# Another order of the seven block products, and of their loads, in the gate and up products of the feed-forward network

## The chip, the cores and the metric

The kernel runs on one core of a Trainium2 chip. The metric is the device time of one execution in microseconds (us). TensorE is called PE in the rows, its weight loads PEld, VectorE DVE, ScalarE ACT, GpSimd POOL and SyncE SP.

## The reference

Two post-norm decoder layers over 512 tokens of width 1024, all in fp32. Each layer has a token mixer (dilated attention beside retention) and then the feed-forward network that this case is about:

```
def _swiglu(x, w_gate, w_up, w_down):
    h = jax.nn.silu(jnp.einsum('bsd,df->bsf', x, w_gate)) * jnp.einsum('bsd,df->bsf', x, w_up)
    return jnp.einsum('bsf,fd->bsd', h, w_down)
...
for l in range(DEPTH):
    mix = _hybrid_mixer(...)
    x = _layer_norm(ALPHA * x + mix, ln1_g[l], ln1_b[l])
    ffn = _swiglu(x, w_ffn_gate[l], w_ffn_up[l], w_ffn_down[l])
    x = _layer_norm(ALPHA * x + ffn, ln2_g[l], ln2_b[l])
```

The hidden width is 2816, which is 22 column blocks of 128.

## The kernel before

Every fp32 product is made from fp32r halves: an operand is cast to a high part (`whi`, ScalarE, line 323), and the low part is what the cast left over (`wlo`, VectorE, line 329). `mm3` then issues three matmuls: high by high, high by low, low by high.

The feed-forward network walks over pairs of column blocks, f = 0, 2, ..., 20. The pair f = 0 is a plain product (`ffn_plain`). The ten others (`ffn_pair`) treat gate and up together as the right half of a 2 x 2 block product: the tokens are halved (256 each) and the 1024 inputs are halved (512 each), so that A11, A12, A21, A22 are blocks of x, B11 and B21 are the two halves of the up weights, and B12 and B22 those of the gate weights. In Winograd's form seven block products do instead of eight:

| product | left | right | running sum in PSUM | what its eviction does |
|---|---|---|---|---|
| M1 | A11 | B11 | A (first) | ScalarE copies A to `sn` (line 1050) |
| M2 | A12 | B21 | X (alone) | VectorE adds X to the copy of M1 |
| M5 | S1 | P1 = B11 + B12 | C (first) | ScalarE copies C |
| M3 | S4 | B22 | C | VectorE subtracts, silu, product, `put` to `ht` |
| M6 | S2 | P2 = P1 + B22 | A | ScalarE copies A |
| M7 | S3 | P3 = B12 + B22 | A | VectorE subtracts from the copy of M5, silu |
| M4 | A22 | P4 = P2 + B21 | A | VectorE multiplies, `put` to `ht` |

Signs are left to the sums S1 to S4 of x, which are made once a layer (`x_sums`). A product is 24 matmuls of 256 columns (two 128-column halves of the weights, four 128-row blocks, three matmuls each). Chain A is one PSUM tile that M1, M6, M7 and M4 add to, so M6 can't write it until M1 has been copied out, and so on; chain C holds M5 and then M3.

The right sides: five loads of 512 KB a call on SP's queue. P1 and P3 are loaded, and the gate block is then added in place by an accumulating DMA that GpSimd issues (line 314). P2 and P4 are VectorE additions in place into P1's buffer (line 340). Raw loads rotate through 8 buffers (`rawp`), `whi` and `wlo` through 4 each (`wp`), PSUM tiles through 8. So the cast for one product waits until the product four ahead of it in the order has left its `whi`.

`ORDER` sets the order of the products and so the order in which `Right` prepares the weights: `operands` casts the next product's right side before the current one's matmuls. A scheduler then places the instructions in each engine's queue; it may pull matmuls of one product between those of another. The pairs are run in three parts (f = 2 and 4; 6 to 12; 14 to 20), and after each part the down product of what it made follows (`xstat`, 512-column matmuls named `ps<-...,ht`).

Of the kernel before, what the change touches and what calls it, by code (L numbers as in the profile page):

```python
# [18 lines left out]
P = 128  # L19
# [34 lines left out]
def hybrid_kernel(ctx, tc, x, rel_bias, w_in, b_in, w_attn_proj, w_ret_proj, w_out,  # L54
# [28 lines left out]
    def mm3(ps, ah, al, bh, bl, start, stop):  # L83
        mm(ps, ah, bh, start, False)
        mm(ps, ah, bl, False, False)
        mm(ps, al, bh, False, stop)

    def psum(name="px"):
        return psm.tile([P, S], F32, tag="mm", name=name)

    def hilo(src, hi, lo):
        act.copy(out=hi, in_=src)  # L92
        dve.tensor_tensor(out=lo, in0=src, in1=hi.bitcast(F32), op=ALU.subtract)  # L93
# [4 lines left out]
    def work(name):  # L98
        return wk.tile([P, S], F32, tag="w2", name=name)

    def rows(w):
        return w.rearrange("(k p) c -> p k c", p=P)
# [4 lines left out]
    def load(src, a, b):  # L107
        v = view(raw(), a, b)
        nc.sync.dma_start(v, src)
        return v  # L110

    def unit(v):
        a, b = v.shape[1], v.shape[2]
        h = view(wp.tile([P, 1024], F32R, tag="whi", name="whi"), a, b)
        l = view(wp.tile([P, 1024], F32R, tag="wlo", name="wlo"), a, b)
        hilo(v, h, l)
        return h, l
# [15 lines left out]
    def tick(us):  # L133

        if side:
            credit[0] += rate[0] * us
            while side and credit[0] >= 1.0:
                credit[0] -= 1.0
                side.popleft()()
# [88 lines left out]
    def wstat(us, q):  # L228

        need(*range(NI))  # L230
        ps = psum("ps")
        for k in range(KD):
            h, l = part_of(us, k, q)
            mm3(ps, h, l, xh[:, k], xl[:, k], k == 0, k == KD - 1)
            tick(STEP)
        return ps
# [41 lines left out]
    def tail_units(raws):  # L278

        out_ = []  # L280
        for j, r in enumerate(raws):
# [12 lines left out]
    ORDER = ((1, "A11", "B11"), (2, "A12", "B21"), (5, "S1", "P1"), (3, "S4", "B22"),  # L294
             (6, "S2", "P2"), (7, "S3", "P3"), (4, "A22", "P4"))
    CHAIN = {1: "A", 6: "A", 7: "A", 4: "A", 2: "X", 5: "C", 3: "C"}
    FIRST = (1, 2, 5)

    class Right:

        def __init__(self, src, shapes):
            self.src, self.shapes, self.t = src, shapes, {}

        def load(self, *names):
            for n in names:
# [24 lines left out]
        def begin(self, n):  # L333

            if n == "B11":
                self.load("B11", "B21", "P1", "P3", "B22")
            elif n in ("P2", "P4"):
                for u in range(len(self.shapes)):
                    r = self.t["P1", u]
                    dve.tensor_tensor(out=r, in0=r, in1=self.t["B22" if n == "P2" else "B21", u], op=ALU.add)  # L340
            return self.high(n)

        def operands(self):

            ahead = self.begin("B11")
            for i in range(len(ORDER)):
                now, low = ahead
                low()
                ahead = self.begin(ORDER[i + 1][2]) if i + 1 < len(ORDER) else None
                yield now  # L350

    def x_left(an, j, ts_):

        if an[0] == "S":
            o_ = xs[:, SN.index(an)]
            return o_[:, 0, j, ts_], o_[:, 1, j, ts_]
        k = j + (4 if an[2] == "2" else 0)
        o = 256 if an[1] == "2" else 0
        t_ = slice(o + ts_.start, o + ts_.stop)
        return xh[:, k, t_], xl[:, k, t_]  # L360

    def tall(right, n, left, ev, bias_=None):
# [3 lines left out]
        for (i, an, bn), units in zip(ORDER, right.operands()):  # L366
            ks = [(u, k) for u in units for k in range(u[0].shape[1])]
            c = CHAIN[i]
            for a in range(2):
                fresh = i in FIRST  # L370
                if fresh:
# [17 lines left out]

    def wide(right, left, ev):  # L390

        ps = {}
        for (i, an, bn), ((h, l),) in zip(ORDER, right.operands()):
            c = CHAIN[i]
            if i in FIRST:
                ps[c] = psum("ps")
            for q in range(2):
                cs = slice(q * P, (q + 1) * P)
                for k in range(4):
                    ah, al = left(an, k, slice(0, 256))  # L400
                    mm3(ps[c][:, q * 256:(q + 1) * 256], h[:, k, cs], l[:, k, cs], ah, al,
                        i in FIRST and q == 0 and k == 0, k == 3)
                    tick(STEP / 2)
            if i != 3:
                ev(i, ps[c])
            if i == 6:
                ev(3, ps["C"])
            yield

    def run(g):  # L410
        for _ in g:
            pass
# [204 lines left out]
    def layer(ly, cp):  # L617
# [197 lines left out]
        with stage("ret") as rp:  # L815
# [93 lines left out]
            for dp in range(KD // 2):  # L909
                sg = []  # L910
                for b, c in enumerate((C_GA, C_GB)):
                    us = pair_units(w_l, c + dp * 256)
                    t = slot("sg", F32)
                    for e in range(2):
                        ps = wstat(us, e)
# [3 lines left out]
                h, l = unit(load(wa_l[:, :, dp * 256:(dp + 1) * 256], NG, 256))  # L919
                if dp == KD // 2 - 1:  # L920
                    drain()
                for e in range(2):
                    cs = slice(e * P, (e + 1) * P)
                    ps = psum("ps")
# [39 lines left out]
        with stage("mp") as mp:  # L964
# [10 lines left out]
            for dp in range(KD // 2):  # L975
# [9 lines left out]
                for hh, (h, l) in enumerate(us):  # L985
                    for e in range(2):
                        cs = slice(e * P, (e + 1) * P)
                        for t in range(4):
                            k = 4 * hh + t
# [28 lines left out]
        wg_l, wu_l, wd_l = rows(w_ffn_gate[ly]), rows(w_ffn_up[ly]), rows(w_ffn_down[ly])  # L1018
# [15 lines left out]

        def ffn_pair(f, o_):

            def src(b, u):
                k = 4 if b[1] == "2" else 0
                return (wg_l if b[2] == "2" else wu_l)[:, k:k + 4, f * P:f * P + 256]

            sn = {}

            def put(v, ts_):
                hilo(v, o_[:, 0, :, ts_], o_[:, 1, :, ts_])

            def ev(i, ps):
                p2 = ps.rearrange("p (q t) -> p q t", q=2)
                if i in (1, 5, 6):
                    sn[i] = work("sn").rearrange("p (q t) -> p q t", q=2)
                    act.copy(out=sn[i], in_=p2)  # L1050
                elif i == 2:
                    dve.tensor_tensor(out=sn[1], in0=p2, in1=sn[1], op=ALU.add)
                elif i == 3:
                    v = sn[6]
                    dve.tensor_tensor(out=v, in0=p2, in1=v, op=ALU.subtract)
                    act.activation(out=v, in_=v, func=AF.Silu)
                    dve.tensor_tensor(out=v, in0=v, in1=sn[1], op=ALU.mult)
                    put(v, slice(0, 256))
                elif i == 7:
                    dve.tensor_tensor(out=sn[5], in0=sn[5], in1=p2, op=ALU.subtract)  # L1060
                    act.activation(out=sn[5], in_=sn[5], func=AF.Silu)
                elif i == 4:
                    v = sn[5]
                    dve.tensor_tensor(out=v, in0=v, in1=p2, op=ALU.mult)
                    put(v, slice(256, 512))

            run(wide(Right(src, [(4, 256)]), x_left, ev))

        for part, (f0, f1) in enumerate(FPARTS):
            ht = []  # L1070
# [89 lines left out]
```

## Time and profile before

| what | value |
|---|---|
| median of 3 runs | 2224.86 us (2223.46 to 2225.05) |
| the profiled execution, its own time | 2224.68 us |
| its span, first to last instruction | 2222.9 us |
| PE busy | 2184.1 us, 98% of the span |
| PEld / DVE / ACT / POOL busy | 85% / 61% / 43% / 11% |
| granted PE clock, mean | 0.998 |
| mean DMA rate | 147 GB/s |

The span and the time of the same execution differ by 1.8 us, which lies before the first and behind the last instruction. A row of the timeline gives start, duration, engine, line, operation and, in brackets, how long the engine had been idle and what ended that. Matmuls overlap in the pipeline, so their rate is read from start to start, and not from their durations.

### The profile page before, as it was taken

How to read it: one execution, taken by the hardware profiler on the slowest of the kernel's cores; microseconds unless marked ns; L12 is line 12 of the kernel's file. 1: busy time of each engine (PE TensorE's matmuls, PEld its weight loads, DVE VectorE, ACT ScalarE, POOL GpSimd, SP SyncE). 2: the span in 40 equal slices, each digit the busy share in tenths (PEclk: the TensorE clock that was granted, in tenths of full speed). 3: DMA queues.
4: the chain of work that ended last, by engine and by line, in shares of the span. 5: the costliest groups of instructions: out<-in, count | busy, mean ns of one | idle time of the engine just before them, and what ended most of it. 6: DMA issues, size and time to landing. Idle time of an engine off the chain costs nothing.

```text
span 2222.9 us, 31189 instructions
## 1 busy us (share of the span) xinstructions
PE 2184.1 (98%) x12330; PEld 1884.7 (85%) x12330; DVE 1352.1 (61%) x1971; ACT 946.8 (43%) x1517; POOL 233.5 (11%) x280
## 2 busy tenths in 40 slices
PE   8999999999999999999999999999999999999998
PEld 7877788888888898989898778888888889899896
DVE  5643677875245675646676447777843357666575
ACT  4444544545333253525245445444543234444350
POOL 3110011100000100000040100111000001010001
PEclk9999999999999999999999999999999999999999
DMA  8944266455656356556269343666455562565551
GB/s 226 238 124 103 63 157 170 132 141 157 207 179 190 85 144 141 161 133 152 86 160 243 105 94 85 151 164 157 130 175 192 185 189 64 160 149 155 128 152 38
DMA packets 293300, 325.92 MB, mean 147 GB/s; under 512 B 22478, under 2 KB 231522, under 8 KB 293025
## 3 DMA queue, kind: packets, MB, share of 16 engines
q1 hardware_dynamic: 223488, 244.62, 36.7%
q0 software_dynamic: 42384, 66.52, 15.4%
q10 hardware_dynamic: 27280, 12.80, 2.0%
q8 instruction: 96, 1.57, 0.3%
q14 instruction: 52, 0.42, 0.1%
HBM read 298.09 MB, written 28.53 MB: 147 GB/s over the span
## 4 chain that ended last, share of the span: by engine, by line
PE 80%; issue 10%; DMA 5%; DVE 3%; ACT 2%; POOL 1%; SPq 0%; POOLq 0%; DVEq 0%; ACTq 0%
PE ps L81 72%; PE px L81 6%; DMA raw<-in_w_in 3%; DVE wlo L329 1%; ACT whi L323 1%; PE px L526 1%; PE px L858 1%; DVE wlo L93 0%; POOL ry L124 0%; DMA rb<-in_b_in 0%; PE px L169 0%; DMA exd<-pk 0%; DVE xtok L951 0%; DMA exd<-wb 0%; ACT whi L92 0%
## 5 line engine op out<-in xcount | busy, mean ns | idle before, releaser
L81 PE MATMUL ps<-xh,whi 128*128 128x512 f32 (+1 forms) x1600 | 562.6, 353 | 5.9 <-ACT whi L92 3.3
L81 PE MATMUL ps<-xh,wlo 128*128 128x512 f32 (+1 forms) x1600 | 546.5, 342 | 10.5 <-DVE wlo L329 9.0
L81 PE MATMUL ps<-xl,whi 128*128 128x512 f32 (+1 forms) x1600 | 544.9, 341 | 0.2 <-DVE xl L93 0.2
L329 DVE TENSOR_TENSOR wlo<-raw,whi 128x1024 fp32r<-128x1024 f32 (+1 forms) x308 | 349.4, 1136 | 183.4 <-ACT whi L323 180.3
L323 ACT CAST whi<-raw 128x1024 fp32r<-128x1024 f32 (+1 forms) x308 | 300.4, 979 | 303.1 <-PE ps L81 176.9
L93 DVE TENSOR_TENSOR wlo<-raw,whi 128x1024 fp32r<-128x1024 f32 (+2 forms) x194 | 232.4, 1200 | 300.1 <-ACT whi L92 299.4
L81 PEld LDWEIGHTS ps<-xh,wlo 128*128 128x128 f32 x1600 | 302.7, 189 | 48.8 <-DVE wlo L329 11.5
L81 PEld LDWEIGHTS ps<-xh,whi 128*128 128x128 f32 x1600 | 302.2, 190 | 46.4 <-issue 6.4
L81 PEld LDWEIGHTS ps<-xl,whi 128*128 128x128 f32 x1600 | 303.8, 190 | 29.0 <-DVE xl L93 1.0
L92 ACT CAST whi<-raw 128x1024 fp32r<-128x1024 f32 (+2 forms) x194 | 198.7, 1031 | 285.4 <-PE ps L81 216.5
L81 PE MATMUL ps<-xs,whi 128*128 128x256 f32 (+1 forms) x1536 | 315.1, 302 | 0.0
L81 PEld LDWEIGHTS ps<-xs,whi 128*128 128x128 f32 x1536 | 248.7, 191 | 13.8 <-ACT sn L1050 3.5
L81 PE MATMUL ps<-xs,wlo 128*128 128x256 f32 (+1 forms) x768 | 229.9, 301 | 0.0
L81 PE MATMUL ps<-whi,xs 128*128 128x512 f32 (+1 forms) x768 | 220.0, 360 | 2.8 <-ACT whi L323 1.6
L81 PE MATMUL ps<-whi,ht 128*128 128x512 f32 x576 | 178.8, 390 | 0.0
L81 PEld LDWEIGHTS ps<-whi,xs 128*128 128x128 f32 x768 | 137.7, 188 | 23.6 <-ACT whi L323 2.4
L81 PEld LDWEIGHTS ps<-xs,wlo 128*128 128x128 f32 x768 | 146.5, 191 | 5.4 <-DVE wlo L329 0.4
L81 PE MATMUL ps<-wlo,xs 128*128 128x512 f32 (+1 forms) x384 | 138.3, 360 | 2.7 <-DVE wlo L329 2.5
L81 PEld LDWEIGHTS ps<-whi,ht 128*128 128x128 f32 x576 | 107.4, 188 | 21.4
L314 POOL DMA_DIRECT2D raw<-in_w_ffn_gate x40 | 51.9, 1298 | 675.8 <-DMA raw<-in_w_ffn_up 378.3
L81 PE MATMUL ps<-wlo,ht 128*128 128x512 f32 x288 | 112.8, 392 | 0.3
L81 PE MATMUL ps<-whi,xh 128*128 128x512 f32 (+1 forms) x288 | 103.5, 359 | 1.4 <-DVE sn L453 1.4
(179 smaller groups left out, 2862.3 us busy)
## 6 DMA issues: line engine op xcount, KB each, us to landing
raw<-in_w_in SPq DMA_DIRECT2D x144, 512.0 KB, 4.1
raw<-in_w_ffn_up SPq DMA_DIRECT2D x64, 512.0 KB, 4.5
raw<-in_w_ffn_gate SPq DMA_DIRECT2D x44, 512.0 KB, 3.8
raw<-in_w_ffn_down SPq DMA_DIRECT2D x44, 512.0 KB, 3.7
raw<-in_w_ffn_gate POOLq DMA_DIRECT2D x40, 512.0 KB, 6.4
raw<-in_w_in SPq DMA_DIRECT2D x72, 256.0 KB, 5.0
raw<-in_w_in POOLq DMA_DIRECT2D x32, 512.0 KB, 8.6
raw<-in_w_ret_proj SPq DMA_DIRECT2D x32, 512.0 KB, 4.0
```

The costliest lines, as they stand in the source:

```text
L81: pe.matmul(ps, lhsT=a, rhs=b, start=start, stop=stop, skip_group_check=True)
L92: act.copy(out=hi, in_=src)
L93: dve.tensor_tensor(out=lo, in0=src, in1=hi.bitcast(F32), op=ALU.subtract)
L314: pool.dma_start(r, self.src({"P1": "B12", "P3": "B22"}[n], u), accum_op=ALU.add)
L323: act.copy(out=h, in_=src)
L329: dve.tensor_tensor(out=l, in0=src, in1=h.bitcast(F32), op=ALU.subtract)
L526: pe.transpose(px[:, (2 + j) * P:(3 + j) * P], s[:, hh, j * P:(j + 1) * P], ident)
L858: pe.transpose(px[:, t * P:(t + 1) * P], ys[i][:, t * P:(t + 1) * P], ident)
```

## The change

The wide form gets an order and an order of loads of its own. For nine of the ten pairs of a layer the products come as M1, M5, M6, M2, M7, M3, M4; for f = 2, M1, M2, M5, M6, M3, M7, M4, because the sums S1 to S4 are then still being made. The loads come as B11, P1, B22, P3, B21 in all ten. Each product's eviction is now called right behind its product; before, that of M3 was called behind M6. The other users of `Right` (the `tall` form) keep their order.

```diff
+    WIDE = tuple(ORDER[i] for i in (0, 2, 4, 1, 5, 3, 6))
+    WIDE1 = tuple(ORDER[i] for i in (0, 1, 2, 4, 3, 5, 6))
...
-        def __init__(self, src, shapes):
-            self.src, self.shapes, self.t = src, shapes, {}
+        def __init__(self, src, shapes, order=ORDER, loads=("B11", "B21", "P1", "P3", "B22")):
+            self.src, self.shapes, self.order, self.loads, self.t = src, shapes, order, loads, {}
...
             if n == "B11":
-                self.load("B11", "B21", "P1", "P3", "B22")
+                self.load(*self.loads)
...
+    def pair_right(w1, w2, c, order=WIDE):
+
+        def src(b, u):
+            k = 4 if b[1] == "2" else 0
+            return (w2 if b[2] == "2" else w1)[:, k:k + 4, c:c + 256]
+
+        return Right(src, [(4, 256)], order, ("B11", "P1", "B22", "P3", "B21"))
...
-        for (i, an, bn), ((h, l),) in zip(ORDER, right.operands()):
+        for (i, an, bn), ((h, l),) in zip(right.order, right.operands()):
...
-            if i != 3:
-                ev(i, ps[c])
-            if i == 6:
-                ev(3, ps["C"])
-            yield
+            ev(i, ps[c])
...
-            run(wide(Right(src, [(4, 256)]), x_left, ev))
+            wide(pair_right(wu_l, wg_l, f * P, WIDE1 if f == 2 else WIDE), x_left, ev)
```

On PE, where one pair call of the second part (running sum A in `ps_7606`) meets the next (`ps_7837`). Right sides here: `whi_7696` is P2, `whi_7724` is P3, `whi_7830` is the next call's B11. Before:

```order
L81 MATMUL ps_7606<-xs_81,wlo_7697 128x256
L81 MATMUL ps_7606<-xs_81,whi_7696 128x256 x2
L81 MATMUL ps_7606<-xs_81,wlo_7697 128x256
L81 MATMUL ps_7837<-xh_79,whi_7830 128x256
L81 MATMUL ps_7837<-xl_80,whi_7830 128x256
L81 MATMUL ps_7837<-xh_79,wlo_7831 128x256
L81 MATMUL ps_7837<-xh_79,whi_7830 128x256
L81 MATMUL ps_7837<-xl_80,whi_7830 128x256
L81 MATMUL ps_7837<-xh_79,wlo_7831 128x256
L81 MATMUL ps_7837<-xh_79,whi_7830 128x256
L81 MATMUL ps_7606<-xs_81,whi_7724 128x256 x2
L81 MATMUL ps_7606<-xs_81,wlo_7725 128x256
```

And now, where `whi_7757` is P4:

```order
L81 MATMUL ps_7606<-xl_80,whi_7757 128x256
L81 MATMUL ps_7606<-xh_79,wlo_7758 128x256
L81 MATMUL ps_7606<-xh_79,whi_7757 128x256
L81 MATMUL ps_7606<-xl_80,whi_7757 128x256
L81 MATMUL ps_7606<-xh_79,wlo_7758 128x256
L81 MATMUL ps_7837<-xh_79,whi_7830 128x256
L81 MATMUL ps_7837<-xl_80,whi_7830 128x256
L81 MATMUL ps_7837<-xh_79,wlo_7831 128x256
```

Before, 7 matmuls of the next call's M1 stood between M6 and M7 of the running call, and 8 more between M7 and M4; in the same way M6 was cut in two (13 and 11) around M3. Now the seven products of these calls follow each other whole, 24 matmuls each, and the next call's M1 stands behind M4.

On ACT, the casts and PSUM copies of the same call. Before (`ps_7667` is chain C; 7664 is B22, 7760 P4):

```order
L1050 COPY sn_7631<-ps_7606 128x512
L323 CAST whi_7696<-raw_7591 128x1024
L323 CAST whi_7724<-raw_7594 128x1024
L323 CAST whi_7760<-raw_7591 128x1024
L1050 COPY sn_7692<-ps_7667 128x512
L323 CAST whi_7830<-raw_7818 128x1024
L323 CAST whi_7834<-raw_7820 128x1024
L1050 COPY sn_7751<-ps_7606 128x512
L1056 ACTIVATE sn_7751<-sn_7751 128x512
```

And now (`ps_7638` is chain C; 7696 is P3, 7726 B22, 7757 P4, 7830 and 7834 the next call's B11 and P1, 7866 its P2):

```order
L325 CAST whi_7696<-raw_7594 128x1024
L1053 COPY sn_7631<-ps_7606 128x512
L325 CAST whi_7726<-raw_7592 128x1024
L1053 COPY sn_7663<-ps_7638 128x512
L325 CAST whi_7757<-raw_7589 128x1024
L1053 COPY sn_7693<-ps_7606 128x512
L325 CAST whi_7830<-raw_7818 128x1024
L325 CAST whi_7834<-raw_7820 128x1024
L1064 ACTIVATE sn_7663<-sn_7663 128x512
L325 CAST whi_7866<-raw_7820 128x1024
```

The copies of M1, M5 and M6 (into `sn_7631`, `sn_7663`, `sn_7693`) now each stand behind one cast, and the next call's B11, whose cast stood ahead of M6's copy, is now cast behind it.

On POOL, in layer 0, where the first layer norm's reciprocal roots (`ry`) meet the accumulating loads of f = 2 and f = 4. Before:

```order
L314 DMA raw_6688<-in_w_ffn_gate 128x4x256
L314 DMA raw_6691<-in_w_ffn_gate 128x4x256
L124 TENSOR_TENSOR ry_6258<-ve_6257,mhalf_76 128x1
L314 DMA raw_6933<-in_w_ffn_gate 128x4x256
L124 TENSOR_TENSOR ry_6297<-ve_6296,mhalf_76 128x1
```

And now:

```order
L316 DMA raw_6686<-in_w_ffn_gate 128x4x256
L316 DMA raw_6691<-in_w_ffn_gate 128x4x256
L316 DMA raw_6931<-in_w_ffn_gate 128x4x256
L124 TENSOR_TENSOR ry_6258<-ve_6257,mhalf_76 128x1
L124 TENSOR_TENSOR ry_6297<-ve_6296,mhalf_76 128x1
```

The accumulating load of f = 4's P1 (`raw_6933` before, `raw_6931` now) has moved from behind the first root to in front of it.

## Rows read from the trace of the kernel before

**Rows 1.** The page, part 4: the chain that ended last, by engine.

```profile
PE 80%; issue 10%; DMA 5%; DVE 3%; ACT 2%; POOL 1%; SPq 0%; POOLq 0%; DVEq 0%; ACTq 0%
```

**Rows 2.** The chain over the second part, layer 0: start us, us, what.

```profile
874.91 15.99 PE ps L81 x131
890.90 3.15 issue
894.05 1.05 ACT whi L323
...
895.13 1.24 DVE wlo L329
...
896.41 15.99 PE ps L81 x131
```

**Rows 3.** TensorE's timeline in that stretch: start us, us, instruction, idle before.

```profile
890.68 0.77 PE L81 MATMUL ps<-xs,whi 128*128 128x256 f32 x3
891.29 0.28 PE L81 MATMUL ps<-xs,wlo 128*128 128x256 f32 x1
...
895.37 0.28 PE L81 MATMUL ps<-xl,whi 128*128 128x256 f32 x1
896.41 0.39 PE L81 MATMUL ps<-xh,wlo 128*128 128x256 f32 x1 [0.75 <-DVE wlo L329]
896.63 0.28 PE L81 MATMUL ps<-xh,whi 128*128 128x256 f32 x1
896.75 0.27 PE L81 MATMUL ps<-xl,whi 128*128 128x256 f32 x1
...
900.93 0.37 PE L81 MATMUL ps<-xh,whi 128*128 128x256 f32 x1
901.14 0.28 PE L81 MATMUL ps<-xl,whi 128*128 128x256 f32 x1
```

**Rows 4.** Windows view of one call: us, each engine's busy us (x instructions), clock, DMA.

```profile
874.91:896.41 21.50, 20.74 (x169) 20.31 (x169) 15.22 (x16) 10.90 (x16) 2.58 (x2) 1.00 0.72 172
```

**Rows 5.** ScalarE's timeline in the same call.

```profile
889.36 1.05 ACT L323 CAST whi<-raw 128x1024 fp32r<-128x1024 f32 x1 [1.83 <-PE ps L81]
890.31 0.58 ACT L1050 COPY sn<-ps 128x512 f32<-128x512 f32 x1
```

**Rows 6.** TensorE's timeline where the first part's down product begins.

```profile
820.67 0.62 PE L81 MATMUL ps<-whi,ht 128*128 128x512 f32 x2
821.36 0.50 PE L81 MATMUL ps<-wlo,ht 128*128 128x512 f32 x1
```

**Rows 7.** Groups by line and shape: busy us, mean ns of one | idle before.

```profile
L329 DVE TENSOR_TENSOR wlo<-raw,whi 128x1024 fp32r<-128x1024 f32 x252 | 307.3, 1222 | 159.2 <-ACT whi L323 156.5
...
L323 ACT CAST whi<-raw 128x1024 fp32r<-128x1024 f32 x252 | 262.9, 1047 | 256.4 <-PE ps L81 151.1 <-issue 76.0 <-ACT whi L323 11.4
...
L340 DVE TENSOR_TENSOR raw<-raw 128x1024 f32<-128x1024 f32 x72 | 87.8, 1220 | 1.5
...
L314 POOL DMA_DIRECT2D raw<-in_w_ffn_gate x40 | 51.9, 1298 | 675.8 <-DMA raw<-in_w_ffn_up 378.3 <-DVE ht L93 96.1 <-DVE wlo L329 95.6
...
L1050 ACT COPY sn<-ps 128x512 f32<-128x512 f32 x60 | 34.8, 581 | 3.9 <-PE ps L81 3.9
```

**Rows 8.** Timelines of VectorE and ScalarE in the call f = 2, layer 0.

```profile
784.84 0.68 DVE L1032 TENSOR_TENSOR sl<-sl,ps 128x512 f32<-128x512 f32 x1
...
787.06 0.59 ACT L1050 COPY sn<-ps 128x512 f32<-128x512 f32 x1 [1.95 <-PE ps L81]
```

**Rows 9.** The page, part 6: DMA issues, KB each, median us to landing.

```profile
raw<-in_w_ffn_up SPq DMA_DIRECT2D x64, 512.0 KB, 4.5
...
raw<-in_w_ffn_gate POOLq DMA_DIRECT2D x40, 512.0 KB, 6.4
```

**Rows 10.** Timelines of SP and GpSimd before the feed-forward network, layer 0.

```profile
731.84 0.37 SPq L109 DMA_DIRECT2D raw<-in_w_ffn_up  x1
...
742.28 1.53 POOL L124 TENSOR_TENSOR ry<-ve,mhalf 128x1 f32<-128x1 f32 x1 [17.50 <-DVE ve L123]
```

More of the change, by code (lines that the diff above doesn't have):

```diff
@@ L345, in operands @@
             ahead = self.begin("B11")
-            for i in range(len(ORDER)):
+            for i in range(len(self.order)):
                 now, low = ahead
                 low()
-                ahead = self.begin(ORDER[i + 1][2]) if i + 1 < len(ORDER) else None
+                ahead = self.begin(self.order[i + 1][2]) if i + 1 < len(self.order) else None
                 yield now
+    def pair_right(w1, w2, c, order=WIDE):
[3 more added lines that the diff above has]
+        return Right(src, [(4, 256)], order, ("B11", "P1", "B22", "P3", "B21"))
     def x_left(an, j, ts_):
@@ L1035, in ffn_pair @@
         def ffn_pair(f, o_):
-            def src(b, u):
-                k = 4 if b[1] == "2" else 0
-                return (wg_l if b[2] == "2" else wu_l)[:, k:k + 4, f * P:f * P + 256]
             sn = {}
```

## The prediction, made before the changed kernel was run

> **What bounds the kernel now.** The page's chain comes first: four fifths of the span is TensorE's [rows 1], so only time in which TensorE stands still can be won, and the question is how much of that lies in the pair calls. The chain over the second part shows it. It repeats every 21.50 us (874.91 to 896.41), one pair call, and each time it leaves TensorE in the same way: to a cast on ScalarE, then a low part on VectorE, then back to TensorE [rows 2]. A call is 168 matmuls. TensorE's timeline says what one costs: from start to start 0.12 us where nothing is waited for (896.63 to 896.75) [rows 3], so a call needs 168 x 0.12 = 20.16 us, and 1.34 us of each 21.50 is standing still.
>
> The timeline says where:
> - at the meeting of two calls 1.04 us lie between two matmuls of the next call's M1 (895.37 to 896.41), and 0.22 before the next, 0.92 + 0.10 too long; and M4, behind eight more of that M1's matmuls, still has to wait for VectorE to have read M7's sum: one step of 0.21 (900.93 to 901.14), 0.09 too long [rows 3]. Together 1.11 us;
> - where M3 adds to chain C, which M5's copy has to leave first, four starts lie 0.61 apart that should take 0.36 (890.68 to 891.29) [rows 3]: 0.25 us.
>
> 1.11 + 0.25 = 1.36, against the 1.34 from the period. Why the first is so long: the `whi` buffer of the next call's B11 is the one that M3 leaves, four ahead. M3 runs late, cut into M6, and the next M1 is pulled forward into the gap behind M6. So the cast can start only at 894.05, and 1.05 of cast and 1.24 of low part follow it [rows 2], while only 11 matmuls of M6 (1.3 us) were left as cover.
>
> The windows view puts PE at 20.74 us busy in the same call [rows 4], 0.76 idle, not 1.34: matmuls overlap, and a busy row runs past the next start. The Trainium skill, Perfetto Trace Analysis, section Tensor Engine Instruction (MATMUL, LD_WEIGHTS), says that a matmul's end in a profile is computed from its size and not observed. The trace agrees, for durations of 0.28 us stand at starts 0.12 apart [rows 3]; by the busy rows the sum below would be little over half as large.
>
> **The change, part by part.** No instruction is added or removed in TensorE's, ScalarE's or VectorE's work; they are placed differently.
>
> *What it takes away.* Now one product of another chain stands between any two products of one chain in nine of ten calls (A: M1, M6, M7, M4; C: M5, then M3 four places on). No matmul of the next call has to be pulled forward, and the order shows whole products. I count the standing time over both layers, from start to start as above. The 0.25 us in each of 20 calls: 5.0. The meeting of two calls: 14 of them (one in the first part, three in each other, times two layers) at 1.11: 15.5. Where a part ends, matmuls of the down product are pulled forward instead: 0.69 for two steps of 0.23 (820.67 to 821.36) [rows 6], 0.23 too long; with the two lengthened steps that such a wait and M4's bring, 0.10 each as in [rows 3], 0.43 in the four places where a part with more to come ends, and one lengthened step in each layer's last part: 1.9. Sum: 22.4.
>
> *What could take its place.* I walk through a call of the new order with its clock at 0 when M1 starts; product n ends at 2.88n. A cast takes 1.05, a low part and an addition 1.22 each, a copy 0.58 [rows 7].
> - M6 (third, starts 5.76) needs M1 copied out. That copy stands behind the cast of P3, which itself waits for the end of M1, as a cast and a copy already do now (0.95 us from one to the other) [rows 5]. 2.88 + 0.2 for the end of the last matmul + 1.05 + 0.58 = 4.7: 1.0 us to spare. The rule that speaks against this order is the Trainium skill's, PSUM — Partial Sum Buffer, section Engine vs sequencer instructions: ScalarE's and VectorE's queues are strictly first in, first out, so a PSUM copy can't pass a cast that waits. By that rule the cast is part of the wait, 1.05 on top of 0.58, and the cover of one product still holds it; without a product between, it would cost 1.8 us where now 0.25 stands.
> - M7 (fifth, 11.52) needs M6 copied out: the cast of P4 waits for M6's end, 8.64 + 0.2 + 1.05 + 0.58 = 10.5: 1.0 to spare. M3 (sixth) has the same copy of M5 done at about 7.6, seven us early.
> - M4 (seventh, 17.28) needs VectorE to have read M7's sum: M7 ends at 14.4, the subtraction is 0.7, and at most one low part stands in front: 16.5, 0.8 to spare.
> - The next call's B11 takes over M2's buffer, free at 11.52: cast, then low part, done by 14.2 with a VectorE wait; needed at 20.16. P1 of the next call takes over M7's, at 14.4: ready by 17, needed at 23.0. P2 is an addition, a cast and a low part (3.5 us) in a row, but begins when P1's low part is done, at 17: ready by 21 with other work between, needed at 25.9.
> - VectorE and ScalarE stay at 15.2 and 10.9 us of work [rows 4] in a call of 20.2.
> - Loads. The fifth buffer, now B21's, is the one that P1 of the call before leaves, and P1's is left last: by P4's low part, 8.64 + 0.2 + 1.05 + 1.22 = 11.1; before, B21's was left by the addition, a cast and a low part sooner. Landing takes 4.5 us [rows 9]: 15.6. B21 is cast after 20.16 at the soonest. The accumulating load of P1 is issued a call ahead, lands 6.4 us later [rows 9], and has over 10 us.
>
> *The call f = 2*, where VectorE also makes S1 to S4. M1 ends at 787.0 (its copy starts at 787.06, waiting for it), so M6, now fourth, would start at 792.8. VectorE's queue up to 784.84 is the same as now [rows 8]; behind it stand a product of 0.68, then the addition for P2, the low part of S2 and that of P2, 3 x 1.22: 789.2. M3 (fifth, 795.6) also needs the subtraction for S4, M2's eviction 0.68, and two low parts: 793.5. M7 needs one more low part: 794.8 against 798.5. Only M4 is tight: M7 ends at 801.4, VectorE is then in a run of low parts, and 20 pulled-forward matmuls (2.4 us) cover it; I put down 0.15 us a layer, between 0 and 1.2.
>
> *GpSimd.* The accumulating load of f = 4's P1 now stands ahead of the first root. Its plain load was issued at 731.84 as the second load and would land at 736.3 [rows 9]; 1.3 us of issue [rows 7] end at 737.6. The root waits for VectorE until 742.28 anyway [rows 10]: 4.7 to spare, nothing.
>
> *Sum.* 2224.7 (the profiled execution) - 22.4 + 0.3 = 2202.6. That execution lies 0.2 below the median of the runs, so 2202.8 as a median.
>
> **The rivals.**
> 1. *Evictions come late, part of the waits comes back.* The margins above are 0.8 to 1.0 us in three places of a call. Were VectorE's subtraction of M7 two low parts behind instead of one, M4 would wait 1.22 - 0.8 = 0.4 us, and with its lost step 0.5 in 20 calls: +10, 2213. For it: VectorE has 15.2 of 20.2 us filled. Against: its queue there has one low part, and that one's cast waits for M2, long over. With half as much in ten calls the time is 2205, which I count here too.
> 2. *Busy rows are right.* If TensorE's rate, not its waits, held the call, half of the gain would go into longer steps: 14 to 20 calls x 0.76 us = 11 to 15 us won, 2210 to 2214. Against: 0.12 is kept over whole products at a granted clock of 1.00 [rows 4].
> 3. *Slower: the fifth load.* SP issues in order, and B21's buffer is now the last one left. If its load took x us, M2 would wait from x = 4.5 + 11 on (landing at 15.6; needed, with cast and low part of 2.3, at 26.5 in the same clock). To lose 22.1 and 4.5 more in 20 calls it takes 1.33 us each, a load of 16.7 us; the median is 4.5 [rows 9]. Then 2229 or more.
> 4. *No change*, 2220 to 2229: the waits move one for one to where the casts wait, which the order, with three products between a buffer's end and its next use, speaks against.
>
> **How the numbers follow.** The forecast, 0.86; rival 1, 0.06; rival 2, 0.03; rival 3, 0.02; rival 4, 0.03. The forecast's own bounds: nothing left standing and 0.4 of run to run, 2201; f = 2 at its upper bound in both layers, 2.4, and as much again for places between the parts that I did not walk, 2206.5. The range reaches into rival 1: 2200.5 to 2209. Less than 0.2% of the time, 4.4 us, is about what a measurement of this kernel can tell from none. Faster: 0.86 + 0.06 + 0.03 = 0.95; same, rival 4: 0.03; slower, rival 3: 0.02.
>
> **What would show it.** In the changed kernel's trace the chain over the second part has no cast and no low part of a right side in it; the period of a call is 20.2 us; no start-to-start step between M5 and M3 or M7 and M4 is over 0.13; the wait of TensorE on a right side's low part, once a call now, is gone. In f = 2 the step into M4 is at most a few tenths. I would be wrong by rival 1 if steps of 0.3 to 0.6 stood in front of M6, M7 or M4 with ScalarE's copy or VectorE's subtraction as releaser, and by rival 3 if the cast of B21 waited for a DMA.

## The result, and the profile after

| | median us | runs |
|---|---|---|
| before | 2224.24 | 2223.46 to 2225.05 |
| after | 2201.37 | 2200.46 to 2203.24 |

The ratio is 0.9898, with a 95% interval of 0.9881 to 0.9915: faster by 1.0%. The profiled execution of after took 2203.24 us, 2201.4 of them span, at a mean granted clock of 0.997. In the table of the experiments one of ten executions of the kernel with the new loads alone, 8224.23 us, is a slow one: it counts in that median and not in the ratio.

The chain that ended last, on the page of after, by engine; it answers to [rows 1]:

```profile
PE 88%; DMA 4%; issue 4%; DVE 2%; ACT 1%; POOL 1%; SPq 0%; POOLq 0%; DVEq 0%; ACTq 0%
```

TensorE has gone from 80% to 88% of the chain, and the share of "issue" from 10% to 4%. The same chain over the second part of layer 0, where [rows 2] left TensorE once in every call, is now one piece (start us, us, what):

```profile
854.79 75.23 PE ps L81 x611
```

One call in the windows view, against [rows 4] (us, busy us of PE, PEld, DVE, ACT, POOL with instructions, granted clock, DMA share, GB/s):

```profile
879.68:899.84 20.16, 20.16 (x170) 20.16 (x169) 15.14 (x17) 10.90 (x15) 3.81 (x3) 1.00 0.81 184
```

The stretch runs from one call's line 1067 to the next one's: a period of 20.16 us, which is 168 x 0.12, at an unchanged clock. TensorE's timeline at the two places that stood still in [rows 3] (start us, us, instruction): the step into M4, and the meeting of two calls:

```profile
875.86 0.28 PE L81 MATMUL ps<-xs,wlo 128*128 128x256 f32 x1
875.98 0.28 PE L81 MATMUL ps<-xh,whi 128*128 128x256 f32 x1
...
878.74 0.28 PE L81 MATMUL ps<-xh,wlo 128*128 128x256 f32 x1
878.86 0.28 PE L81 MATMUL ps<-xh,whi 128*128 128x256 f32 x1
```

Both steps are 0.12. I count the standing time as the prediction did, every step from one 256-column start to the next beyond 0.12 us in the pair calls, and beyond 0.23 for 512 columns where the parts end: 11.35 us in each layer before, 0.16 in each layer after.

ScalarE's timeline in the same call, which starts at 858.70 (M4's start above, 875.98, less the 17.28 of six products), and VectorE's read of M7:

```profile
861.70 1.05 ACT L325 CAST whi<-raw 128x1024 fp32r<-128x1024 f32 x1 [1.70 <-PE ps L81]
862.66 0.58 ACT L1053 COPY sn<-ps 128x512 f32<-128x512 f32 x1
...
867.46 1.05 ACT L325 CAST whi<-raw 128x1024 fp32r<-128x1024 f32 x1 [1.35 <-issue]
868.42 0.58 ACT L1053 COPY sn<-ps 128x512 f32<-128x512 f32 x1
870.30 1.05 ACT L325 CAST whi<-raw 128x1024 fp32r<-128x1024 f32 x1 [1.30 <-PE ps L81]
```

```profile
871.38 1.23 DVE L331 TENSOR_TENSOR wlo<-raw,whi 128x1024 fp32r<-128x1024 f32 x1 [0.27 <-ACT whi L325]
873.30 0.69 DVE L1063 TENSOR_TENSOR sn<-sn,ps 128x512 f32<-128x512 f32 x1 [0.70 <-PE ps L81]
```

The copies of M1 and M6 each stand behind a cast that waits for the end of the same product (for M6 the row names no releaser; the cast starts 0.12 us after M6's 24 matmuls end at 867.34), and still end 1.22 us before M6 (864.46) and M7 (870.22) want the tile. The next call's B11 is cast at 870.30, the moment M2 leaves its buffer, and its low part is done at 872.61: 6.25 us before 878.86. In the kernel before it was done at the moment it was wanted [rows 2].

The one wait that is left, in f = 2 at M4; TensorE's timeline, then VectorE's:

```profile
805.14 0.28 PE L81 MATMUL ps<-xl,whi 128*128 128x256 f32 x1
805.31 0.38 PE L81 MATMUL ps<-xh,whi 128*128 128x256 f32 x1
805.54 0.28 PE L81 MATMUL ps<-xl,whi 128*128 128x256 f32 x1
```

```profile
803.98 0.68 DVE L93 TENSOR_TENSOR ht<-sn,ht 128x512 fp32r<-128x512 f32 x1
804.58 0.68 DVE L1063 TENSOR_TENSOR sn<-sn,ps 128x512 f32<-128x512 f32 x1
```

VectorE comes to M7's sum late, behind a run of other work, is done with it at 805.26, and TensorE's steps are 0.17 and 0.23: 0.16 us too long.

### The profile page after: what moved, and what is told of

Same layout as the page of the kernel before. It is cut to its first block, busy times and chain, and to the rows that moved or that the text cites. A ratio compares the mean times of both kernels' runs of the same rounds, so it can differ in the third digit from the quotient of the medians.

```text
span 2201.4 us, 31211 instructions
## 1 busy us (share of the span) xinstructions
PE 2175.8 (99%) x12330; PEld 1886.4 (86%) x12330; DVE 1351.9 (61%) x1971; ACT 947.0 (43%) x1517; POOL 233.6 (11%) x280
## 4 chain that ended last, share of the span: by engine, by line
PE 88%; DMA 4%; issue 4%; DVE 2%; ACT 1%; POOL 1%; SPq 0%; POOLq 0%; DVEq 0%; ACTq 0%
PE ps L81 80%; PE px L81 6%; DMA raw<-in_w_in 3%; PE px L533 1%; PE px L865 1%; PE px L169 0%; POOL ry L124 0%; DMA exd<-pk 0%; DMA exd<-wb 0%; DMA mb<-exd 0%; DMA rb<-in_b_in 0%; DVE xtok L958 0%; DVE wlo L331 0%; DMA fa<-exd 0%; ACT xh L92 0%
## 5 line engine op out<-in xcount | busy, mean ns | idle before, releaser
L81 PEld LDWEIGHTS ps<-whi,ht 128*128 128x128 f32 x576 | 108.1, 188 | 22.4
```

Source lines behind the costliest of these rows:

```text
L81: pe.matmul(ps, lhsT=a, rhs=b, start=start, stop=stop, skip_group_check=True)
```

## The experiments

My theory: two things made the standing time, the rotation of the `whi` buffers at the meeting of two calls and neighbours on one PSUM chain inside a call, and the order of the products takes both away; the order of the loads does nothing. The rivals: the loads have a part in it; only the rotation counts; neighbours on a chain are what costs, whatever the buffers do.

All ratios are to the kernel before, run beside it on the same chip.

| kernel | median us | ratio, 95% interval |
|---|---|---|
| after with the old loads | 2199.81 | 0.9899 (0.9882 to 0.9916) |
| before with the new loads | 2223.37 | 1.0004 (0.9994 to 1.0013) |
| f = 2's order in all calls | 2202.68 | 0.9906 (0.9891 to 0.9921) |
| before, own buffer for B11 | 2234.89 | 1.0050 (1.0032 to 1.0069) |
| the same from f = 4 on | 2212.58 | 0.9943 (0.9926 to 0.9959) |
| after, M6 beside M7 | 2204.14 | 0.9908 (0.9893 to 0.9923) |
| after, casts twice | 2209.10 | 0.9933 (0.9913 to 0.9952) |
| after, casts three times | 2310.18 | 1.0383 (1.0366 to 1.0400) |
| after, new order in the first head too | 2192.92 | 0.9859 (0.9845 to 0.9874) |
| after, new order in all heads | 2193.67 | 0.9862 (0.9847 to 0.9877) |
| after, again | 2199.81 | 0.9888 (0.9873 to 0.9903) |

**The products alone, and the loads alone.** The first kernel is after with one argument gone:

```diff
-        return Right(src, [(4, 256)], order, ("B11", "P1", "B22", "P3", "B21"))
+        return Right(src, [(4, 256)], order)
```

> The changed kernel with the old order of loads (B11, B21, P1, P3, B22); the products keep their new order. My theory, that the order of the products alone takes the waits away: 2201 to 2203 us, as the changed kernel, period of a call 20.16 us; every load lands well before its cast, whichever comes first. Rival, that the loads give a part: over 2204 us, with a cast or an accumulating load that ends a wait on TensorE in front of M5 or M6.

The second is before with the new loads:

```diff
-                self.load("B11", "B21", "P1", "P3", "B22")
+                self.load(*self.loads)
...
+        return Right(src, [(4, 256)], ORDER, ("B11", "P1", "B22", "P3", "B21"))
```

> The kernel before with the new order of loads (B11, P1, B22, P3, B21); products and evictions keep their old order. My theory: nothing waits for a load, so 2223 to 2226 us, as before, period of a call 21.50 us. Rival, that the loads give a part: under 2220 us. Slower would mean that M2, second in this order, now waits for B21, the last load.

The products alone give the whole gain (2199.81 is 1.2 us under the range that I had put down, but the ratio is that of after), the loads alone nothing. With the order of the products goes the place where M3's eviction is called; no run has one without the other. The chain of the second kernel over the second part of layer 0 (start us, us, what) still leaves TensorE as [rows 2] did, with the same lengths to 0.01 us:

```profile
865.51 3.15 issue
868.65 1.06 ACT whi L325
...
869.74 1.24 DVE wlo L331
...
871.02 16.00 PE ps L81 x131
```

**The rotation alone.** Before, with its old orders, and one more buffer, so that B11 need not wait for M3 (the other four are then shared by six products and not seven, so the whole rotation is looser):

```diff
-                h = view(wp.tile([P, 1024], F32R, tag="whi", name="whi"), a, b)
-                l = view(wp.tile([P, 1024], F32R, tag="wlo", name="wlo"), a, b)
+                own = own_wp[0] if n == "B11" and len(self.shapes) == 1 else wp
+                h = view(own.tile([P, 1024], F32R, tag="whi", name="whi"), a, b)
+                l = view(own.tile([P, 1024], F32R, tag="wlo", name="wlo"), a, b)
...
+        own_wp[0] = fin.enter_context(stage("wb"))
```

> The kernel before, all orders as they were, but the right side B11 of a pair call has a whi and a wlo buffer of its own, so that its cast need not wait for M3 to leave one. My theory, that the long wait at the meeting of two calls comes from the rotation through four buffers: 14 x (0.92 + 0.10) = 14.3 us and about 1 us at the part ends go, the 0.25 us at M3 in 20 calls and the step into M4 stay: 2207 to 2211 us, period of a call 20.4 to 20.6 us. Rival, that the neighbours on chain A (M6, M7, M4) cause it and the buffer only happens to be late: 2221 to 2225 us.

It was slower than before, against every expectation. The view of TensorE's waits over layer 0's pair calls (what waited, for what: us in total, times, longest) gives the main reason:

```profile
PE ps L81 <- ACT whi L325: 7.8, 1, 7.8
```

That is one wait, in f = 2, at 791.2; layer 1 has the same at 1892.6. Behind it the granted clock was 0.51 (791.10 to 795.70), and the next 19 steps took 2.3 us more than 0.12 each. In the later calls the wait at the meeting is gone, as the theory has it, but 0.59 us a call are left. So the extra buffer went to f = 4 and later only:

```diff
-        own_wp[0] = fin.enter_context(stage("wb"))
+        wb = fin.enter_context(stage("wb"))
...
+            own_wp[0] = wb if f > 2 else wp
             run(wide(Right(src, [(4, 256)]), x_left, ev))
```

> The kernel before with whi and wlo buffers of its own for B11, but only in the calls f = 4 to 20; f = 2 shares the four buffers as before, so that its cast does not wait for space that an earlier stage holds. In the kernel with the extra buffer in every call the standing time of a steady call was 0.59 us (0.15 + 0.10 before M3, 0.15 + 0.10 before M7, 0.09 before M4) where the kernel before has 1.36. My theory, that the rotation makes 0.77 us of a call and the neighbours on a chain the rest: 16 to 18 calls of 0.6 to 0.8 us less, 2210 to 2214 us. Rival, that the rotation did not matter and only f = 2 was unlucky: 2221 us or more.

2212.58, as expected. (The long wait went with the buffer in f = 2; that it was for space which an earlier stage still held is only argued. The cast that ended it stood in ScalarE's queue behind two casts of f = 0's `ht`.) What is left, in TensorE's timeline of one call, before M3, before M7 and before M4:

```profile
887.56 0.78 PE L81 MATMUL ps<-xs,whi 128*128 128x256 f32 x3
888.18 0.28 PE L81 MATMUL ps<-xs,wlo 128*128 128x256 f32 x1
...
893.57 0.28 PE L81 MATMUL ps<-xh,whi 128*128 128x256 f32 x1
893.84 0.51 PE L81 MATMUL ps<-xs,whi 128*128 128x256 f32 x2
894.18 0.28 PE L81 MATMUL ps<-xs,wlo 128*128 128x256 f32 x1
...
897.77 0.37 PE L81 MATMUL ps<-xh,whi 128*128 128x256 f32 x1
897.98 0.28 PE L81 MATMUL ps<-xl,whi 128*128 128x256 f32 x1
```

Three steps in 0.62 for 0.36, three in 0.61 for 0.36, one in 0.21 for 0.12: 0.60 us, and by the period (887.56 to 908.30, 20.74) 0.58. The first and the last stood before too [rows 3]. The middle one, M7 waiting for the copy of M6, which ends at 893.79, is new: before, TensorE was by then already held up at the meeting. So of 1.35 us in a call the rotation is worth 0.76 and the neighbours on a chain 0.59, and in the time 2224.44 - 2212.58 = 11.9 us and 2212.58 - 2199.81 = 12.8 us (medians from one chip). In the traces the stretches from f = 0 to the end of a layer, both layers together, give 9.2 and 13.4; with the extra buffer the first part's end stands 0.7 us a layer longer than before. Neither of the one-cause rivals stands.

**Neighbours on a chain, one pair at a time.** First M7 beside M4, with the order of f = 2 everywhere:

```diff
-            wide(pair_right(wu_l, wg_l, f * P, WIDE1 if f == 2 else WIDE), x_left, ev)
+            wide(pair_right(wu_l, wg_l, f * P, WIDE1), x_left, ev)
```

> The changed kernel with the order of the call f = 2 (M1, M2, M5, M6, M3, M7, M4) in all ten calls of a layer. M7 and M4 follow each other on chain A, and eight matmuls of the next call's M1 are pulled in between. My theory: the short lengthened step into M4 comes back, 0.1 to 0.15 us in 18 more calls, 2203.5 to 2205 us; the next B11's buffer is the one that M6 leaves, three products ahead of the call's end, so no wait of a microsecond at the meeting of two calls. Rival, that any two neighbours on one chain cost the 1.1 us seen before: 2221 us or more.

Then M6 beside M7:

```diff
-    WIDE = tuple(ORDER[i] for i in (0, 2, 4, 1, 5, 3, 6))
+    WIDE = tuple(ORDER[i] for i in (0, 2, 1, 4, 5, 3, 6))
```

> The changed kernel with M2 moved ahead of M6 in nine of the ten calls of a layer: M1, M5, M2, M6, M7, M3, M4. Now M6 and M7 follow each other on chain A; the scheduler pulls 13 matmuls of M3 in between them, and 11 stay between M7 and M4. My theory, that the buffer rotation and not the neighbourhood made the long wait: the 13 matmuls (1.56 us) cover the copy of M6 (0.2 + 0.58, no waiting cast ahead of it), and the 11 (1.3 us) leave at most 0.1 to 0.3 us in front of M4: 2202 to 2207 us. Rival, that neighbours on one chain cost about 1.1 us a call whatever the buffers do: 2218 us or more.

2202.68 is 0.8 us under its range and 2204.14 in its range, but the intervals overlap with that of after, and the times alone would not tell them from it. Their traces do. In the first the step into M4 is 0.09 to 0.10 us too long in the nine calls behind f = 2, with f = 2's 0.15 it makes 0.97 us in each layer, and nothing else stands: the small price that was expected, and no 1.1 us. In the second, ScalarE's timeline and TensorE's:

```profile
887.28 1.05 ACT L325 CAST whi<-raw 128x1024 fp32r<-128x1024 f32 x1 [1.83 <-PE ps L81]
888.24 0.58 ACT L1053 COPY sn<-ps 128x512 f32<-128x512 f32 x1
```

```profile
888.60 0.78 PE L81 MATMUL ps<-xs,whi 128*128 128x256 f32 x3
889.21 0.28 PE L81 MATMUL ps<-xs,wlo 128*128 128x256 f32 x1
```

0.25 us stand in front of M7 in all 18 calls, 4.5 in sum, and nothing in front of M4. The expectation had the place wrong: it said that no waiting cast is ahead of M6's copy. One is: it starts 0.12 us behind M6's 24 matmuls (887.16), and the copy ends 1.54 us after the cast's start, at 888.82, where 13 matmuls of M3 cover 1.56. Those 0.12 us make the difference: M7's first matmul is 0.15 us late, the one behind it 0.10. This is the rule that the prediction weighed, from the Trainium skill, PSUM — Partial Sum Buffer, section Engine vs sequencer instructions: ScalarE's queue is strictly first in, first out, so a copy can't pass a cast that waits. This trace agrees: the copy starts 0.96 us after the cast, though M6's end released both.

**How much cover the new order has.** After, with every cast of a pair call done two and three times into the same buffer, which changes nothing of what is computed (here two; `range(3 ...)` for three):

```diff
-                act.copy(out=h, in_=src)
+                for _ in range(2 if len(self.shapes) == 1 else 1):
+                    act.copy(out=h, in_=src)
```

> The changed kernel with every cast of a pair call's right side done twice, into the same buffer: about 0.95 us more of ScalarE in front of the copies of M1, M5 and M6. My theory, that M6 and M7 have 1.0 us to spare because the copy stands behind one cast: the margin is just used up, 0 to 0.15 us of wait in two places of a call, 2201 to 2207 us. Rival, that ScalarE's copy has no cast in front of it when it counts: no change at all here and none with a third cast.

> The changed kernel with every cast of a pair call's right side done three times: about 1.9 us more of ScalarE in front of each copy. My theory, with 1.0 us to spare at M6 and at M7: 0.9 us of wait at each of the two in some 18 calls, 32 us, 2230 to 2240 us, with ScalarE's copy of M1 and of M6 as releaser of TensorE. Rival, that the margin is larger or the cast not in front: under 2210 us.

With two casts a steady call loses nothing. The windows view of one:

```profile
879.90:900.06 20.16, 20.16 (x171) 20.16 (x170) 15.07 (x17) 17.48 (x21) 2.56 (x2) 1.00 0.75 179
```

But the run does not do what I expected of it. In ScalarE's timeline, and TensorE's where M7 begins:

```profile
887.86 2.00 ACT L326 CAST whi<-raw 128x1024 fp32r<-128x1024 f32 x2
889.76 0.59 ACT L1054 COPY sn<-ps 128x512 f32<-128x512 f32 x1
890.24 4.16 ACT L326 CAST whi<-raw 128x1024 fp32r<-128x1024 f32 x4
```

```profile
892.11 0.40 PE L81 MATMUL ps<-xs,whi 128*128 128x256 f32 x2
```

M2's 24 matmuls lie between, so M6 ends at 889.23. The two casts ahead of its copy start 1.4 us before that and do not wait for it; the copy ends at 890.35, 1.76 us before M7 wants the tile. That is more to spare than after's 1.22 and not less, because the scheduler now placed the copy ahead of the cast that waits for M6. So this run does not test the margin; M6's copy had no waiting cast in front, as the rival has it.

The time still grew, by 7.7 us over after's 2201.37. By the count of steps 4.9 and 4.8 us are too long in the two layers, all in f = 2, where ScalarE also casts the sums, and at one place of f = 4, which I had not counted; 1.5 and 1.4 of them are steps at a lower clock (last section). With three casts I expected two waits of 0.9; measured were 6.6 us a call:

```profile
901.90:928.70 26.80, 22.47 (x169) 21.86 (x170) 15.52 (x17) 23.89 (x29) 2.56 (x2) 0.94 0.63 141
```

ScalarE is busy for 23.89 of 26.80 us. I had reckoned with margins only, and not with the sum: 10.90 and 14 more casts of 0.95 are 24.2 us, more than the 20.16 of a call. ScalarE became the bound, and this run says nothing on the margin of a copy.

**The new order where the program had kept the old.** The `tall` form (a product of the retention heads' values and gates) has the same seven products, each right side in two loads. After, with the new orders there in the first head of each layer, and each eviction called behind its product:

```diff
...
-            yield from biased(halves(w_l, 0, (2, 2), cv, cg, RV), RV, rows_, left, gate)
+            yield from biased(halves(w_l, 0, (2, 2), cv, cg, RV, *((WIDE, ("B11", "P1", "B22", "P3", "B21")) if h == 0 else ())), RV, rows_, left, gate)
```

> The changed kernel with the new order of products and loads also in the tall form of the first retention head of each layer, whose right sides come as two loads each. Standing time there in the changed kernel is 2.3 us in layer 0. My theory: the order takes away what neighbours on a chain cost, 1 to 2.5 us a layer at most, 2197 to 2201 us. Rival: the ten loads of this form do not fit into eight raw buffers, the last ones come later than now, and the time is the same or up to 6 us longer.

In all heads (the condition on `h` gone), and after itself again on that chip:

> As the kernel with the new order in the tall form of the first retention head, but in all four retention heads of both layers. With the first head alone 2192.9 us were measured (ratio 0.9859 to the kernel before). In the changed kernel the tall forms of heads 2 to 4 stand for only about 0.05 us each, so my theory is no further gain: 2191 to 2195 us. Rival, that ten loads in eight raw buffers hold the casts up in the later heads, where no attention work fills in: 2196 us or more.

> The changed kernel again, beside the two others on one chip. Both theories: 0.990 of the kernel before, 2200 to 2203 us; the difference to the kernel with the new order in the tall forms as well shows what that brings on the same chip.

The first head alone gives 2192.92 us, 4 us under the range that I had put down, and all heads the same; after run again took 2199.81, 0.2 under its range. Against after run again, the ratio of the first head alone differs by 0.0029, 6.5 us; the two intervals just touch (up to 0.9874, from 0.9873). Every execution with all heads (2192.37 to 2196.35) was shorter than every one of after beside it (2197.48 to 2202.18). The waits of TensorE in after (run again) between 190 and 300 us, layer 0 (us in total, times, longest):

```profile
PE px L533 <- ACT s L525: 1.1, 1, 1.1
PE ps L81 <- DVE sn L460: 1.0, 2, 0.8
PE ps L81 <- ACT sn L453: 0.8, 1, 0.8
PE px L81 <- ACT sT L534: 0.7, 1, 0.7
```

With the new order in the first head the same view of the same stretch lists none. Two of the four (lines 460 and 453) are the `tall` form's own chain waits, which I had counted. The other two stand ahead of that product, in the attention; why they went too I have not followed. In layer 1 after (run again) has 2.1 us of the same waits between 1280 and 1380; with all heads 0.4 of them (line 533) is left there, and 0.2 stands at a new place in layer 0. The kernel with the first head alone has none of the four, but two short new waits in layer 1:

```profile
PE px L865 <- ACT yb L860: 0.5, 2, 0.3
```

This version beats both kernels of the case.

## Why the prediction was right

- *The rate, 0.12 us a matmul and 20.16 a call.* Measured 20.16. That the busy rows hide standing time (rival 2) shows in the windows: TensorE's busy time in a call fell from 20.74 [rows 4] to 20.16, so 0.58 of the 1.34 us had lain inside busy rows.
- *The sum, 22.4 us away and 0.3 left in f = 2.* By the same count 22.70 - 0.31 = 22.4, and 0.16 a layer in f = 2, where 0.15 was put down, at the place that was named, M4. That size was not worked out, only chosen between 0 and 1.2: that it fits is luck.
- *Why the meeting of two calls was long.* The buffer was the cause, but with one step unseen: with the buffer free, M7's wait for M6's copy, 0.25, comes out from behind it. The sum did not depend on this, since the order takes both away.
- *The walk through a call* (clock from M1's start, predicted and read): M1's copy done 4.7 and 4.54; M6's 10.5 and 10.30; VectorE done with M7 16.5 and 15.29, since no low part stands in front of it; the next B11 ready 14.2 and 13.91. The margins at M6 and M7 are 1.22 where 1.0 was worked out, and M4's is 1.99 where 0.8 was: rival 1 was further off than I had it. No run tests the margin at M6 and M7 by itself, since the doubled casts moved the copies. The nearest is M6 beside M7: 1.56 us of cover were 0.15 short there, so 1.71 of the 2.88 us of a product are needed, 1.17 to spare.
- *The loads and GpSimd, nothing.* On the page of after, the two kinds of [rows 9] land in:

```profile
raw<-in_w_ffn_up SPq DMA_DIRECT2D x64, 512.0 KB, 4.3
...
raw<-in_w_ffn_gate POOLq DMA_DIRECT2D x40, 512.0 KB, 6.7
```

  No TensorE wait in the pair calls goes back to one of them (rival 3), and either order of the loads gives the same time.
- *The time.* 2202.6 was worked out for the profiled execution, 2203.24 measured; 2202.8 for the median, 2201.37 measured. The profiled executions differ by 21.4 us and not by 22.1: from f = 0 to the end of each layer they differ by 11.2 and 11.5, 22.7 in all, but the stretch ahead, where only the order of loads changed, on SP and GpSimd, was 1.6 us longer in the second one (the first silu of f = 0 at 777.7 and at 779.3), and the stretch between the layers 0.4 shorter. The same kernel run again has that silu at 777.3, so the 1.6 us are not the change's; its median was 2199.81.
- *The bounds.* The terms named for them do not give them: without the 0.3 of f = 2 and 0.4 of run to run the sum is 2202.1 and not 2201, and with twice 2.4 in place of the 0.3 it is 2207.3 and not 2206.5. So 2201.37 lies 0.7 under what the terms give, and the term that was too small is the 0.4: the four executions of after spread over 2.8 us. The range, 2200.5 to 2209, was wide enough.

## What to carry to other kernels

Between two products that add to one PSUM tile, put a whole product of another tile: the copy that must come first stands in its engine's queue behind whatever waits there, and here copy and waiting cast together were 1.54 us, which half a product did not quite cover and a whole one covers with 1.2 to spare. (With doubled casts the scheduler put the copy ahead of the waiting cast; a kernel that does only that was not run.) Where buffers rotate, look which product leaves the one that the next stage needs first; an order that ends with late use of that buffer costs at every meeting. Waits cover each other, so taking one away may show the next (0.25 us behind 1.02): price a cure by a run that applies it alone, add up an engine's whole work, not only its margins, before slowing it, and look in the trace whether a run moved something else as well.

## What the runs showed of the hardware

After longer stands the granted clock was lower. With three casts TensorE stood 2.90 and 0.76 us; its timeline, and a window behind that (clock: third number from the end):

```profile
928.51 0.50 PE L81 MATMUL ps<-xs,whi 128*128 128x256 f32 x2 [2.90 <-ACT whi L326]
929.77 0.39 PE L81 MATMUL ps<-xs,wlo 128*128 128x256 f32 x1 [0.76 <-DVE wlo L332]
...
931.21 0.41 PE L81 MATMUL ps<-xs,wlo 128*128 128x256 f32 x1
931.42 0.63 PE L81 MATMUL ps<-xs,whi 128*128 128x256 f32 x2
931.85 0.41 PE L81 MATMUL ps<-xs,wlo 128*128 128x256 f32 x1
```

```profile
930.70:933.80 3.10, 3.10 (x17) 3.10 (x16) 1.50 (x2) 2.49 (x3) 0.00 (x0) 0.50 0.26 39
```

Three matmuls take 0.64 us, 0.213 each, in place of 0.36, at a granted clock of 0.50: the lower of the two levels, 1.2 GHz. Some 16 steps ran so, 1.5 us more a call. With two casts shorter stands did the same in f = 2: TensorE was idle for 1.34 us before the matmul at 792.65 and for 0.76 before that at 793.91. The window behind them:

```profile
794.80:798.00 3.20, 3.20 (x17) 3.20 (x17) 2.59 (x3) 2.17 (x3) 0.00 (x0) 0.51 0.44 136
```

A stand of 0.75 us alone, in the calls of the kernel before [rows 3], left the clock at 1.00 [rows 4].
